# Second weight halves cast and subtracted later, the triangular inverse with two result buffers and two block loads, attention's suffix sums 0.03 of a period later

## Chip, core and metric

One core of a Trainium2 chip runs the whole program. The metric is the device time of one launch in microseconds (us); three runs of the kernel before gave 1783.5, 1784.86 and 1788.74, median 1784.86.

## What is computed

One inference step of a two-layer hybrid encoder on 512 prompt tokens and 32 sample tokens (544 columns in all), model width 1024, inner width 2048. Layer 0 is an RWKV-7 time mixer: projections of the shifted stream to r, k, v and z, a data-dependent decay, and per head (32 heads of 64) the state recurrence

```
S_t = S_(t-1) diag(w_t) - (S_(t-1) kk_t)(kk_t * a_t)^T + v_t k_t^T ;  y_t = S_t r_t
```

with a group norm, a bonus term, a SiLU gate and an output projection. Its output gives one shared key and value set. Layer 1 is stick-breaking attention with 16 heads of 128, strictly causal:

```
A[t,s] = sigmoid(z_ts) * prod over s<j<t of (1 - sigmoid(z_tj))
```

computed in log space: the suffix sums of log(1 - sigmoid) are matrix products with a triangular matrix.

## The kernel before

**Precision.** Each projection in float32 is three matmuls on a high and a low part: weight high by x high, weight high by x low, weight low by x high. The parts of a weight are made on the chip: SP loads half a column block (512 of the 1024 rows, `wraw`, four buffers), ScalarE (ACT) casts it (`whi`, line 231), and VectorE (DVE) in layer A, or GpSimd (POOL) in layer B, subtracts (`wlo`, line 232). `wsplit` takes the next of three pairs of `whi`/`wlo` buffers in a ring during layer A, so a cast waits until TensorE (PE) has done the last matmul that reads that buffer.

**Order.** All work from the recurrence on is put on an agenda: `at(t, fn)` with t in periods, one period per pair of heads in layer A (16 pairs, three stages of successive pairs overlapping) and one per head in layer B. `flush` sorts the agenda by t, and each engine gets its instructions in that order and runs them in that order. So t sets places in queues, not times. A pair's period is some 38 us in layer A; a head's is some 31 us in layer B. A few entries have small offsets in a table `SHIFT`.

**Layer A, per pair.** `plan_load` (line 530) puts the two loads of a weight block at t and t + 0.3 d, and the two splits (cast and subtract) at t + d and t + 1.47 d, d = 0.17. For the key weights (`q.kw`, t = p - 0.95) that is 0.22 and 0.30 of the period before pair p's, for the value weights (`q.vw`, t = p + 0.55) 0.72 and 0.80. `plan_proj` puts 16 quanta of three matmuls (line 560) over a slot: keys in p - 0.5 to p, values in p + 1 to p + 1.5. `plan_c` is the recurrence over chunks of 64 tokens in eight steps, each x, u, s a twenty-fourth of a period apart: x (line 907 on PE, `xs` line 918 on DVE, `sgc` line 922 on ACT), u (line 929 on PE, `vu` lines 932 and 933 on ACT), s (line 944 on PE, state `st` line 952 on DVE). Between these PE runs the quanta of the projections.

**The triangular inverse.** The recurrence needs the inverses of small unit lower triangular matrices. `plan_b` stores four 32 x 32 block sets to DRAM (`nd`, line 741, due at 0.62), loads them back with one matrix per partition (`npt`, line 754, three loads at 0.70), and POOL does 31 steps of a multiply and an add (lines 771 and 776, due from 0.79 to 1.62) in `qp`, which starts as the identity: `init` (line 764, at 0.78) copies it from `qinit`, filled once by three loads. The result goes to DRAM (`qd`, line 757, at 1.635) and from there back into `lm` (`fetch`, line 745, at 1.73). `plan_m` (transposes `mt`, line 791, on DVE; matmuls 797 and 807) uses it from 1.86 on. All transfers named here are issued by SP, in agenda order. `decays2` (line 596) makes the chunk-end decays `gc` with two small POOL copies from `gx`.

**Layer B, per head.** `plan_att`: logits, six steps of soft-plus per block of scores (last step `spl`, line 1617, DVE), then `tails` (line 1633, PE: matmuls of `sph` and `spl` with the triangle), `add` (line 1637, DVE), `weigh` (line 1640, ACT), `values` (lines 1656 to 1661, PE), and the gates (lines 1667 and 1671, DVE). PE fills in with the quanta of the next head's key, value and query projections. `split_oz` makes the parts for the output projection.

Of the kernel before, what the change touches and what calls it, by code (L numbers as in the profile page):

```python
# [9 lines left out]
F32 = mybir.dt.float32  # L10
# [13 lines left out]
DEC = 32  # L24
# [63 lines left out]
def tile_encoder(ctx: ExitStack, tc: tile.TileContext, i, o):  # L88
# [366 lines left out]
    V.tensor_scalar(out=ka1, in0=vecs["k_a"], scalar1=-1.0, scalar2=1.0, op0=ALU.mult, op1=ALU.add)  # L455
    qg = const.tile([P, 1], F32, name="qg")
    V.tensor_scalar(out=qg, in0=vecs["q_gain"], scalar1=float(P ** -0.5), scalar2=None, op0=ALU.mult)
    qinit = const.tile([108, 11, 32], F32, name="qinit")

    def identity_rows():  # L460

        idd = dram.tile([33, 32], F32, name="idd")
        SY.dma_start(idd, ident[0:33, 0:32])
        for g in range(3):
            SY.dma_start(
                qinit[36 * g:36 * g + 36],
                idd.rearrange("(i g) t -> g i t", g=3)[g:g + 1].broadcast_to([36, 11, 32]))

    def last_rows():
        hl = p1b.tile([P, 2, NK], F32, name="hl")  # L470
# [62 lines left out]
            fn(*args)  # L533
        agenda.clear()

    def plan_load(idx, t, d=0.17):

        parts = wready[idx] = [None, None]

        def load(kh):  # L540
            parts[kh] = wfetch(idx, kh)

        def split_w(kh):
            parts[kh] = wsplit(parts[kh])
        for kh in range(2):
            at(t + 0.3 * d * kh, load, kh)
            at(t + d + 0.47 * d * kh, split_w, kh)

    def plan_proj(x, idx, t0, t1, evac):

# [20 lines left out]
    def plan_a(q):  # L571
# [24 lines left out]
        def decays2():  # L596
            A.activation(q.sg, q.sg, AF.Exp, scale=KAPPA)
            q.gc = wk.tile([P, NCH], F32, tag="gc", name="gc", bufs=4)
            G.tensor_copy(q.gc[:, 0:NCH - 1], q.gx[:, 0:NCH - 1, C])
            G.tensor_copy(q.gc[:, NCH - 1:NCH], q.gx[:, NCH - 1, DEC:DEC + 1])  # L600
        at(t0 - 0.32, decays2)

        def rscaled():
# [126 lines left out]
    def plan_b(q):  # L730

        t0 = q.p
        nd, qd = nd_d[q.p], qd_d[q.p]

        def nblock(hd, b):
            r0 = 64 * (1 - hd) + 32 * b
            return q.lm[r0:r0 + 32, hd, :, 0, 32 * b:32 * b + 32]

        def store(hd, b):
            m = (2 * hd + b) * NCH  # L740
            SY.dma_start(nd[m:m + NCH].rearrange("c s t -> s c t"), nblock(hd, b))

        def fetch(hd, b):
            m = (2 * hd + b) * NCH
            SY.dma_start(nblock(hd, b), qd[m:m + NCH, 0:32].rearrange("c s t -> s c t"))
        for hd in range(2):
            for b in range(2):
                at(t0 + 0.62, store, hd, b)
                at(t0 + 1.73, fetch, hd, b)

        def load(g):
            if g == 0:
                q.npt = wk.tile([108, 32, 32], F32, tag="npt", name="npt")
            SY.dma_start(q.npt[36 * g:36 * g + 36], nd)

        def out(g):
            SY.dma_start(qd.rearrange("m (i g) t -> g m i t", g=3)[g], q.qp[36 * g:36 * g + 36])
        for g in range(3):
            at(t0 + 0.70, load, g)
            at(t0 + 1.635, out, g)  # L760

        def init():
            q.qp = wk.tile([108, 11, 32], F32, tag="qp", name="qp")
            G.tensor_copy(q.qp, qinit)
        at(t0 + 0.78, init)

        def row(j):
            ni, nt = j // 3 + 1, 31 - j
            tmp = wk.tile([108, 11, 32], F32, tag="qtmp", name="qtmp")
            q.tt = tmp[:, 0:ni, 0:nt]  # L770
            G.tensor_tensor(q.tt, q.npt[:, j, j + 1:32].unsqueeze(1).broadcast_to([108, ni, nt]),  # L771
                            q.qp[:, 0:ni, j:j + 1].broadcast_to([108, ni, nt]), ALU.mult)

        def add(j):
            ni = j // 3 + 1
            G.tensor_tensor(q.qp[:, 0:ni, j + 1:32], q.qp[:, 0:ni, j + 1:32], q.tt, ALU.add)  # L776
        b0, b1 = t0 + 0.79, t0 + 1.62
        for j in range(31):
            at(b0 + (b1 - b0) * (2 * j) / 62, row, j)
            at(b0 + (b1 - b0) * (2 * j + 1) / 62, add, j)  # L780
# [388 lines left out]
    at(1.02, open_b)  # L1169
    for p, q in enumerate(pairs):  # L1170
        if p >= 2:
            plan_load(q.kw, p - 0.95)
        if p >= 1:
            plan_load(q.vw, p + 0.55)
        for plan in (plan_a, plan_lm, plan_b, plan_m, plan_v, plan_c, plan_d):
            plan(q)

# [387 lines left out]
    def plan_att(q):  # L1565
# [78 lines left out]
            for step in range(6):  # L1644
                at(t0 + 0.185 + 0.07 * n + 0.03 * step, soft, b, step)
        for n, b in enumerate((2, 1, 0)):
            at(t0 + 0.53 + 0.035 * n, tails, b)
            at(t0 + 0.565 + 0.035 * n, add, b)
            at(t0 + 0.60 + 0.035 * n, weigh, b)
        out = {}  # L1650

        def values(n):
# [7 lines left out]
            TE.matmul(out["s"][:, :DEC], q.cv, z[2][:, 256:288], start=True, stop=False)  # L1660
            TE.matmul(out["s"][:, :DEC], q.v[:, 4], z[2][:, 288:320], start=False, stop=True)
        for n in range(4):
            at(t0 + 0.72 + 0.02 * n, values, n)
        at(t0 + 0.80, svalues)

        def gate():
            V.tensor_tensor(oz[:, j, 0:SEQ], out["p"], q.z[:, 0:SEQ], ALU.mult)  # L1667
        at(t0 + 0.83, gate)

        def sgate():  # L1670
            V.tensor_tensor(oz[:, j, SEQ:T], out["s"][:, :DEC], q.z[:, SEQ:T], ALU.mult)
        at(t0 + 0.85, sgate)

    def plan_xb():
        st = {}
# [56 lines left out]
        A.copy(hi, oz[:, j, :])  # L1732
        (V if j >= 8 else G).tensor_tensor(out=lo, in0=oz[:, j, :], in1=hi.bitcast(F32), op=ALU.subtract)  # L1733
    for j in range(NE):
        at(NE - 1 - third + 0.02 + 0.04 * j if j < 8 else NE - 1 + 0.02 + 0.04 * (j - 8) if j < NE - 1 else NE - 1 + 0.88,
           split_oz, j)
    with tc.manual_schedule():
        flush()
# [57 lines left out]
```

## Time and profile before

| | |
|---|---|
| runs, us | 1783.5, 1784.86, 1788.74 |
| the profiled execution, us | 1785.67 |
| its span, us | 1784.0 |
| mean granted clock of PE | 0.982 |
| busy: PE, weight loads, DVE, ACT, POOL | 94%, 81%, 43%, 50%, 38% |
| DMA: moved, share of 16 engines | 203.75 MB, 38.2% |
| layer A's steady part | about 270 to 770 us of the span |
| layer B's heads | about 1190 to 1690 us of the span |

Times in the rows are from the start of the span. In a timeline row come the start, the length of the piece, the engine, the line, the operation with tiles and shape, how many were merged (x4), and in brackets how long the engine had been idle before it and whose result ended that idle time. SPq is SP's queue of transfers; its lengths are the time to issue them. PE counts as busy while matmuls are under way, so small waits between them show as idle time of under a microsecond.

### The profile page before, as it was taken

The numbers are of one execution on the slowest core, as the hardware profiler recorded it, in microseconds if no ns is written. First come the engines' busy times: TensorE is split into PE (matmuls) and PEld (weight loads), VectorE is DVE, ScalarE is ACT, GpSimd is POOL, SyncE is SP. The second block draws the span as 40 slices with busy tenths as digits, with TensorE's granted clock in tenths as the row PEclk, the third lists the DMA queues.
The fourth block names the chain that finished last, engine by engine and source line by source line (L and its number), as shares of the span: only waits on it lengthen the run. The fifth ranks groups of instructions, "written<-read, shape, count | busy, mean of one in ns | idle before, by whom it ended". The sixth has DMA issues, their size and how long they took to land. (4 is left out here: it accounts for less than half of the span.)

```text
span 1784.0 us, 38442 instructions
## 1 busy us (share of the span) xinstructions
PE 1675.3 (94%) x15107; PEld 1444.3 (81%) x15107; DVE 765.6 (43%) x1564; ACT 884.9 (50%) x2232; POOL 681.4 (38%) x1371
## 2 busy tenths in 40 slices
PE   5999979999999999999989998999999999999899
PEld 2679867777777777778868998998888888888798
DVE  3674445545555545552355223123443434334400
ACT  2555545565565556555443335254554545555521
POOL 1000276656667666663002443432222222222432
PEclk8999989999999999989999999999999999999999
DMA  8457522333232333332585443433233232323232
GB/s 326 154 160 233 180 76 69 108 84 86 73 80 73 107 80 93 94 89 66 178 287 148 125 142 91 139 106 110 63 85 88 66 107 58 98 75 103 78 111 79
DMA packets 302612, 203.75 MB, mean 114 GB/s; under 512 B 79726, under 2 KB 271872, under 8 KB 300256
## 3 DMA queue, kind: packets, MB, share of 16 engines
q1 hardware_dynamic: 302432, 201.30, 38.2%
q8 instruction: 119, 1.95, 0.5%
q14 instruction: 61, 0.50, 0.1%
HBM read 155.28 MB, written 45.96 MB: 113 GB/s over the span
## 5 line engine op out<-in xcount | busy, mean ns | idle before, releaser
L560 PE MATMUL mm<-x,whi 128*128 128x272 f32 x3584 | 798.4, 315 | 7.0 <-DVE x L1274 3.5
L560 PEld LDWEIGHTS mm<-x,whi 128*128 128x128 f32 x3584 | 572.0, 191 | 70.7 <-issue 23.3
L232 POOL TENSOR_TENSOR wlo<-wraw,whi 128x512 fp32r<-128x512 f32 x198 | 255.2, 1299 | 702.1 <-ACT whi L231 702.1
L560 PE MATMUL mm<-x,wlo 128*128 128x272 f32 x1792 | 520.8, 291 | 1.7 <-POOL wlo L232 1.7
L560 PEld LDWEIGHTS mm<-x,wlo 128*128 128x128 f32 x1792 | 341.3, 190 | 2.4 <-POOL wlo L232 2.4
L231 ACT CAST whi<-wraw 128x512 fp32r<-128x512 f32 x324 | 195.1, 618 | 138.1 <-issue 78.4
L771 POOL TENSOR_TENSOR qtmp<-npt,qp 108x84 f32<-108x84 f32 (+23 forms) x496 | 194.0, 391 | 77.9 <-DMA npt<-nd_d 38.4
L776 POOL TENSOR_TENSOR qp<-qp,qtmp 108x84 f32<-108x84 f32 (+23 forms) x496 | 194.7, 393 | 37.9
L232 DVE TENSOR_TENSOR wlo<-wraw,whi 128x512 fp32r<-128x512 f32 x126 | 88.9, 707 | 116.3 <-ACT whi L231 114.6
L260 PE MATMUL mm<-x,whi 128*128 128x272 f32 x512 | 101.2, 293 | 2.8 <-POOL x L1733 1.4
L932 ACT COPY vu<-ch 64x64 f32<-64x64 f32 (+1 forms) x128 | 27.5, 215 | 133.7 <-PE ch L929 133.4
L952 DVE SCALAR_TENSOR_TENSOR st<-ch,gc,sgc 128x64 f32<-128x64 f32 x128 | 35.7, 279 | 128.2 <-PE ch L944 125.0
L260 PEld LDWEIGHTS mm<-x,whi 128*128 128x128 f32 x512 | 81.7, 190 | 3.9 <-POOL x L1733 1.8
L560 PE MATMUL mm<-xrh,whi 128*128 128x272 f32 x240 | 73.0, 304 | 1.6 <-ACT rout L1087 1.4
L260 PE MATMUL mm<-x,wlo 128*128 128x272 f32 x256 | 74.5, 291 | 0.0
L260 PE MATMUL mm<-yh,whi 128*128 128x272 f32 x256 | 73.9, 288 | 0.0
L260 PE MATMUL mm<-yh,wlo 128*128 128x272 f32 x256 | 73.8, 288 | 0.0
L260 PE MATMUL mm<-yl,whi 128*128 128x272 f32 x256 | 73.8, 288 | 0.0
L560 PE MATMUL mm<-xrh,wlo 128*128 128x272 f32 x240 | 69.3, 289 | 0.3 <-DVE wlo L232 0.3
L560 PE MATMUL mm<-xrl,whi 128*128 128x272 f32 x240 | 69.1, 288 | 0.0
L922 ACT ACTIVATE sgc<-st,gc 128x64 f32<-128x64 f32 x112 | 38.7, 346 | 46.6 <-DVE st L952 46.2
L1640 ACT ACTIVATE z<-z 128x512 f32<-128x512 f32 (+1 forms) x48 | 27.8, 579 | 68.1 <-DVE z L1637 68.1
(322 smaller groups left out, 3180.0 us busy)
## 6 DMA issues: line engine op xcount, KB each, us to landing
wraw<-in_a_w_in_dram SPq DMA_DIRECT2D x128, 256.0 KB
wraw<-in_kv_w_dram SPq DMA_DIRECT2D x68, 256.0 KB
wraw<-in_b_w_in_dram SPq DMA_DIRECT2D x64, 256.0 KB
rca<-rca_d SPq DMA_DIRECT2D x16, 816.0 KB
rca_d<-sgat SPq DMA_DIRECT2D x16, 544.0 KB
x<-in_a_ada_w_dram SPq DMA_DIRECT2D x8, 1024.0 KB
adaw<-in_b_ada_w_dram SPq DMA_DIRECT2D x8, 1024.0 KB
wraw<-in_a_w_out_dram SPq DMA_DIRECT2D x32, 256.0 KB
```

Of the source, the lines that this page charges most:

```text
L231: A.copy(hi, raw)
L232: (V if onV[0] else G).tensor_tensor(out=lo, in0=raw, in1=hi.bitcast(F32), op=ALU.subtract)
L260: TE.matmul(ps[:, :HT], a[:, k % KH, :], b[:, k, s], start=n == 0, stop=n == total - 1)
L560: TE.matmul(ps[half][:, :HT], a[:, k % KH, :], b[:, k, s], start=k + n == 0, stop=k == NK - 1 and n == 2)
L771: G.tensor_tensor(q.tt, q.npt[:, j, j + 1:32].unsqueeze(1).broadcast_to([108, ni, nt]), q.qp[:, 0:ni, j:j + 1].broadcast_to([108, ni, nt]) ...
L776: G.tensor_tensor(q.qp[:, 0:ni, j + 1:32], q.qp[:, 0:ni, j + 1:32], q.tt, ALU.add)
L922: A.activation(sg, state[c], AF.Copy, scale=q.gc[:, c:c + 1])
L932: A.copy(q.vu[64:128, cs, 0, :], pu[64:128, 0:64 * m].rearrange("p (m t) -> p m t", m=m))
L952: V.scalar_tensor_tensor(new, src, gc, ps["g", c], ALU.mult, ALU.add)
L1640: A.activation(z[b][:, :width[b]], z[b][:, :width[b]], AF.Exp)
```

## The change

- `plan_load` takes an optional due time for the second half's split. Key weights: 0.30 becomes 0.43 of the period (p - 0.70 becomes p - 0.57); value weights: 0.80 becomes 0.895. Loads and first halves stay.
- `qp` gets two buffers; `init` moves from 0.78 to 0.52 and becomes three SP loads of the identity from DRAM (`idd`) straight into `qp`, for each of the 16 pairs; the constant `qinit`, its three loads and the POOL copies go.
- `npt` becomes two tiles of 16 rows each, filled by three loads at 0.70 and three at 0.75 (the offset of the old third load no longer applies).
- The two `gc` copies go from POOL to ACT.
- In layer B tails, add, weigh, values and gates are due 0.025 to 0.03 later, and the last head's `split_oz` with them.

```diff
@@ -455,16 +455,10 @@
     V.tensor_scalar(out=ka1, in0=vecs["k_a"], scalar1=-1.0, scalar2=1.0, op0=ALU.mult, op1=ALU.add)
     qg = const.tile([P, 1], F32, name="qg")
     V.tensor_scalar(out=qg, in0=vecs["q_gain"], scalar1=float(P ** -0.5), scalar2=None, op0=ALU.mult)
-    qinit = const.tile([108, 11, 32], F32, name="qinit")
+    idd = dram.tile([33, 32], F32, name="idd")
 
     def identity_rows():
-
-        idd = dram.tile([33, 32], F32, name="idd")
         SY.dma_start(idd, ident[0:33, 0:32])
-        for g in range(3):
-            SY.dma_start(
-                qinit[36 * g:36 * g + 36],
-                idd.rearrange("(i g) t -> g i t", g=3)[g:g + 1].broadcast_to([36, 11, 32]))
 
     def last_rows():
         hl = p1b.tile([P, 2, NK], F32, name="hl")
@@ -533,7 +527,7 @@
             fn(*args)
         agenda.clear()
 
-    def plan_load(idx, t, d=0.17):
+    def plan_load(idx, t, d=0.17, second=None):
 
         parts = wready[idx] = [None, None]
 
@@ -544,7 +538,7 @@
             parts[kh] = wsplit(parts[kh])
         for kh in range(2):
             at(t + 0.3 * d * kh, load, kh)
-            at(t + d + 0.47 * d * kh, split_w, kh)
+            at(second if kh and second else t + d + 0.47 * d * kh, split_w, kh)
 
     def plan_proj(x, idx, t0, t1, evac):
 
@@ -596,8 +590,8 @@
         def decays2():
             A.activation(q.sg, q.sg, AF.Exp, scale=KAPPA)
             q.gc = wk.tile([P, NCH], F32, tag="gc", name="gc", bufs=4)
-            G.tensor_copy(q.gc[:, 0:NCH - 1], q.gx[:, 0:NCH - 1, C])
-            G.tensor_copy(q.gc[:, NCH - 1:NCH], q.gx[:, NCH - 1, DEC:DEC + 1])
+            A.copy(q.gc[:, 0:NCH - 1], q.gx[:, 0:NCH - 1, C])
+            A.copy(q.gc[:, NCH - 1:NCH], q.gx[:, NCH - 1, DEC:DEC + 1])
         at(t0 - 0.32, decays2)
 
         def rscaled():
@@ -748,27 +742,32 @@
                 at(t0 + 0.62, store, hd, b)
                 at(t0 + 1.73, fetch, hd, b)
 
-        def load(g):
+        def load(h, g):
+
             if g == 0:
-                q.npt = wk.tile([108, 32, 32], F32, tag="npt", name="npt")
-            SY.dma_start(q.npt[36 * g:36 * g + 36], nd)
+                q.npt = getattr(q, "npt", []) + [wk.tile([108, 16, 32], F32, tag=f"npt{h}", name=f"npt{h}")]
+            SY.dma_start(q.npt[h][36 * g:36 * g + 36], nd[:, 16 * h:16 * h + 16, :])
 
         def out(g):
             SY.dma_start(qd.rearrange("m (i g) t -> g m i t", g=3)[g], q.qp[36 * g:36 * g + 36])
         for g in range(3):
-            at(t0 + 0.70, load, g)
+            at(t0 + 0.70, load, 0, g)
+            at(t0 + 0.75, load, 1, g)
             at(t0 + 1.635, out, g)
 
         def init():
-            q.qp = wk.tile([108, 11, 32], F32, tag="qp", name="qp")
-            G.tensor_copy(q.qp, qinit)
-        at(t0 + 0.78, init)
+
+            q.qp = wk.tile([108, 11, 32], F32, tag="qp", name="qp", bufs=2)
+            for g in range(3):
+                SY.dma_start(q.qp[36 * g:36 * g + 36],
+                             idd.rearrange("(i g) t -> g i t", g=3)[g:g + 1].broadcast_to([36, 11, 32]))
+        at(t0 + 0.52, init)
 
         def row(j):
             ni, nt = j // 3 + 1, 31 - j
             tmp = wk.tile([108, 11, 32], F32, tag="qtmp", name="qtmp")
             q.tt = tmp[:, 0:ni, 0:nt]
-            G.tensor_tensor(q.tt, q.npt[:, j, j + 1:32].unsqueeze(1).broadcast_to([108, ni, nt]),
+            G.tensor_tensor(q.tt, q.npt[j // 16][:, j % 16, j + 1:32].unsqueeze(1).broadcast_to([108, ni, nt]),
                             q.qp[:, 0:ni, j:j + 1].broadcast_to([108, ni, nt]), ALU.mult)
 
         def add(j):
@@ -1169,9 +1168,9 @@
     at(1.02, open_b)
     for p, q in enumerate(pairs):
         if p >= 2:
-            plan_load(q.kw, p - 0.95)
+            plan_load(q.kw, p - 0.95, second=p - 0.57)
         if p >= 1:
-            plan_load(q.vw, p + 0.55)
+            plan_load(q.vw, p + 0.55, second=p + 0.895)
         for plan in (plan_a, plan_lm, plan_b, plan_m, plan_v, plan_c, plan_d):
             plan(q)
 
@@ -1644,9 +1643,9 @@
             for step in range(6):
                 at(t0 + 0.185 + 0.07 * n + 0.03 * step, soft, b, step)
         for n, b in enumerate((2, 1, 0)):
-            at(t0 + 0.53 + 0.035 * n, tails, b)
-            at(t0 + 0.565 + 0.035 * n, add, b)
-            at(t0 + 0.60 + 0.035 * n, weigh, b)
+            at(t0 + 0.56 + 0.035 * n, tails, b)
+            at(t0 + 0.595 + 0.035 * n, add, b)
+            at(t0 + 0.625 + 0.035 * n, weigh, b)
         out = {}
 
         def values(n):
@@ -1660,16 +1659,16 @@
             TE.matmul(out["s"][:, :DEC], q.cv, z[2][:, 256:288], start=True, stop=False)
             TE.matmul(out["s"][:, :DEC], q.v[:, 4], z[2][:, 288:320], start=False, stop=True)
         for n in range(4):
-            at(t0 + 0.72 + 0.02 * n, values, n)
-        at(t0 + 0.80, svalues)
+            at(t0 + 0.75 + 0.02 * n, values, n)
+        at(t0 + 0.83, svalues)
 
         def gate():
             V.tensor_tensor(oz[:, j, 0:SEQ], out["p"], q.z[:, 0:SEQ], ALU.mult)
-        at(t0 + 0.83, gate)
+        at(t0 + 0.86, gate)
 
         def sgate():
             V.tensor_tensor(oz[:, j, SEQ:T], out["s"][:, :DEC], q.z[:, SEQ:T], ALU.mult)
-        at(t0 + 0.85, sgate)
+        at(t0 + 0.88, sgate)
 
     def plan_xb():
         st = {}
@@ -1732,7 +1731,7 @@
         A.copy(hi, oz[:, j, :])
         (V if j >= 8 else G).tensor_tensor(out=lo, in0=oz[:, j, :], in1=hi.bitcast(F32), op=ALU.subtract)
     for j in range(NE):
-        at(NE - 1 - third + 0.02 + 0.04 * j if j < 8 else NE - 1 + 0.02 + 0.04 * (j - 8) if j < NE - 1 else NE - 1 + 0.88,
+        at(NE - 1 - third + 0.02 + 0.04 * j if j < 8 else NE - 1 + 0.02 + 0.04 * (j - 8) if j < NE - 1 else NE - 1 + 0.91,
            split_oz, j)
     with tc.manual_schedule():
         flush()
```

## Rows read from the trace of the kernel before

**Rows 1.** The page's first part: busy time, share of the span and number of instructions of each engine.
```profile
PE 1675.3 (94%) x15107; PEld 1444.3 (81%) x15107; DVE 765.6 (43%) x1564; ACT 884.9 (50%) x2232; POOL 681.4 (38%) x1371
```

**Rows 2.** The list of waits of PE over the whole span: who waited for whom, us in total, how often, the longest.
```profile
PE at L1633 <- DVE spl L1617: 9.1, 15, 0.6
PE aux L797 <- DVE mt L791: 7.9, 15, 5.3
```

**Rows 3.** The same list for 300 to 760 us, twelve periods of layer A.
```profile
PE ch L907 <- DVE st L952: 17.4, 13, 1.5
PE aux L797 <- DVE mt L791: 2.3, 12, 0.2
```

**Rows 4.** Timeline of one period of layer A around the old place of the key weights' second split, ACT, DVE and PE.
```profile
499.33 0.62 ACT L231 CAST whi<-wraw 128x512 fp32r<-128x512 f32 x1 [0.51 <-PE mm L560]
499.34 0.34 PE L944 MATMUL ch<-vu,kbt 128*64 128x64 f32 x4
...
499.98 0.69 DVE L232 TENSOR_TENSOR wlo<-wraw,whi 128x512 fp32r<-128x512 f32 x1 [1.15 <-ACT whi L231]
...
500.59 0.88 DVE L666 TENSOR_TENSOR rk<-rca,k 128x544 f32<-128x544 f32 x1
501.39 0.27 DVE L952 SCALAR_TENSOR_TENSOR st<-ch,gc,sgc 128x64 f32<-128x64 f32 x1
...
501.72 0.33 PE L907 MATMUL ch<-st,ar 64*64 64x64 f32 x4 [1.35 <-DVE st L952]
```

**Rows 5.** Timeline of PE, the same matmul in three other periods.
```profile
270.47 0.33 PE L907 MATMUL ch<-st,ar 64*64 64x64 f32 x4 [1.41 <-DVE st L952]
...
424.36 0.33 PE L907 MATMUL ch<-st,ar 64*64 64x64 f32 x4 [1.51 <-DVE st L952]
...
463.76 0.33 PE L907 MATMUL ch<-st,ar 64*64 64x64 f32 x4 [1.33 <-DVE st L952]
```

**Rows 6.** Three stretches of the span: their bounds, their length, busy time (and instructions) of PE, PE's weight loads, DVE, ACT and POOL, PE's granted clock as a share of full speed, the DMA engines' busy share, GB/s.
```profile
271.50:274.90 3.40, 3.40 (x32) 2.86 (x29) 1.29 (x2) 0.41 (x2) 2.84 (x12) 0.50 0.93 285
425.00:428.40 3.40, 3.40 (x36) 2.86 (x34) 1.68 (x4) 0.41 (x2) 2.85 (x10) 0.52 0.60 152
...
657.20:660.60 3.40, 3.40 (x36) 2.83 (x35) 1.07 (x2) 0.42 (x2) 2.77 (x11) 0.50 0.85 268
```

**Rows 7.** Timeline of the same period as Rows 4, around the new place of the key weights' second split.
```profile
504.24 0.21 ACT L933 COPY vu<-ch 64x64 f32<-64x64 f32 x1
...
505.51 0.28 DVE L952 SCALAR_TENSOR_TENSOR st<-ch,gc,sgc 128x64 f32<-128x64 f32 x1 [1.05 <-PE ch L944]
...
505.65 0.19 ACT L958 COPY yr<-aux 128x32 f32<-128x32 f32 x1 [1.20 <-PE aux L980]
...
506.10 0.33 PE L907 MATMUL ch<-st,ar 64*64 64x64 f32 x4
```

**Rows 8.** Timeline of the same period, around the old and the new place of the value weights' second split.
```profile
518.14 0.21 ACT L933 COPY vu<-ch 64x64 f32<-64x64 f32 x1
...
518.69 0.34 PE L944 MATMUL ch<-vu,kbt 128*64 128x64 f32 x4
...
519.33 0.69 DVE L232 TENSOR_TENSOR wlo<-wraw,whi 128x512 fp32r<-128x512 f32 x1 [3.10 <-ACT whi L231]
...
520.59 0.97 DVE L791 STREAM_TRANSPOSE mt<-lm 32x288 f32<-32x288 f32 x2
...
521.61 0.75 PE L797 MATMUL aux<-mt,lm 32*32 32x32 f32 x34 [0.19 <-DVE mt L791]
...
522.67 0.21 ACT L932 COPY vu<-ch 64x64 f32<-64x64 f32 x1 [1.86 <-PE ch L929]
...
524.02 0.28 DVE L952 SCALAR_TENSOR_TENSOR st<-ch,gc,sgc 128x64 f32<-128x64 f32 x1 [2.01 <-PE ch L944]
```

**Rows 9.** Timeline of SP's queue and of POOL in the same period: the inverse's transfers and its first step.
```profile
504.41 1.15 SPq L221 DMA_DIRECT2D wraw<-in_a_w_in_dram  x2
509.24 2.47 SPq L741 DMA_DIRECT2D nd_d<-lm  x4
511.81 2.52 SPq L757 DMA_DIRECT2D qd_d<-qp  x3
514.51 1.24 SPq L754 DMA_DIRECT2D npt<-nd_d  x3
516.17 1.97 SPq L745 DMA_DIRECT2D lm<-qd_d  x4
...
519.63 0.49 POOL L771 TENSOR_TENSOR qtmp<-npt,qp 108x31 f32<-108x31 f32 x1 [2.92 <-DMA npt<-nd_d]
```

**Rows 10.** The instructions of the tile `qinit`: shortest, median and longest issue in ns, first and last start in us.
```profile
L465 SPq DMA_DIRECT2D qinit<-idd x3: 342/430/435, 63.5 to 64.4; - x3
```

**Rows 11.** Timeline of the first pair's inverse: the last transfers and PE's wait for them.
```profile
245.82 1.81 SPq L745 DMA_DIRECT2D lm<-qd_d  x4
...
250.13 1.57 PE L797 MATMUL aux<-mt,lm 32*32 32x32 f32 x36 [5.27 <-DVE mt L791]
```

**Rows 12.** Timeline of PE in one head of layer B: the last quantum ahead of the suffix sums, and their first two matmuls.
```profile
1234.53 0.41 PE L560 MATMUL mm<-x,whi 128*128 128x272 f32 x2
...
1234.90 0.38 PE L1633 MATMUL at<-sph,ntri 128*128 128x256 f32 x1
1235.88 0.39 PE L1633 MATMUL at<-spl,ntri 128*128 128x256 f32 x1 [0.60 <-DVE spl L1617]
```

## The prediction

> **What bounds the kernel now.** I read the busy table first. PE is under way 94% of the span and no other engine comes to 51% [rows 1], so time goes only where PE waits, or where its clock falls. Next the list of PE's waits, whole and for the twelve steady periods of layer A. Two entries there belong to the parts that this change touches most: in layer A the matmul of line 907 waits for the state `st` for 17.4 us, 13 times, of which one is small (about 0.1) and twelve are 1.3 to 1.5 [rows 3]; in layer B the suffix sums wait 9.1 us for `spl` in 15 heads [rows 2]. The wait of line 797 for `mt` is 0.19 a period [rows 3], 7.9 in all with one of 5.3 in the first pair [rows 2].
>
> Then the timeline around one of the twelve, to see who is late [rows 4]. PE's matmul 944 for the state is over at 499.68. `st` could follow at once, but in DVE's queue ahead of it stands the subtraction of the key weights' second half. It idles 1.15 us for ACT's cast, and the cast itself had idled 0.51 us until PE had read the last of the buffer that it overwrites. So DVE, free at 498.83, does the subtraction from 499.98, then `rk` (0.88), and `st` only at 501.39; PE stands from 500.37 to 501.72. This is a wait for a buffer that has grown through two queues.
>
> Last the clock. Right after some of these waits (270.47, 424.36 [rows 5]) the granted clock is about 0.5, 1.2 GHz, for 3.4 us with PE busy throughout: I found one after the wait at 270 us and three in the steady part, first and last shown [rows 6]. From 424.36 to 463.76 [rows 5], a period with such a stretch, it takes 39.40 us; from 463.76 to 501.72 [rows 4], one without, 37.96. A stretch costs 1.44.
>
> **The change part by part.**
>
> *Key weights' second half, 0.30 to 0.43.* It now stands behind the copies of step u(3) on ACT and behind the masks on DVE, ahead of `st` of s(3). At the old place DVE does `rk` at 498.83 and `st` at about 499.7, done before 500.37, so PE does not wait: twelve waits, 17.3 us, and the one at 270.47 (pair 3's block), 1.41 [rows 3, 5]: 18.7 us. The blocks of pairs 0 and 1 keep their own due times and are not counted. At the new place ACT is free at 504.45 and would idle 1.20 [rows 7]; the buffer has been free since 499.3. Cast 0.62 [rows 4], so DVE subtracts from 505.07 to 505.76, and `st`, now at 505.51, comes at 505.76 and ends at 506.03; PE wants it at 506.10 [rows 7]. What is queued behind the split is just this `st`, and who waits for it is line 907. The margin is 0.07. Bounds: nothing, and a subtraction in full, 0.69 in each of 13 periods, 9.0. I take 0.05 each, 0.6 us, since the rows put the end ahead of the need.
>
> *The clock.* Without the waits I expect the four stretches that followed them to go: 4 x 1.44 = 5.8 us. Bounds 0 and 5.8. I take the upper, because the stretches start within a microsecond of the end of such a wait and the waits of 0.2 us that stay are a seventh as long.
>
> *Value weights' second half, 0.80 to 0.895.* Before, DVE idled 3.10 us for this cast, then subtracted for 0.69 at 519.33, and `st`, the first product and the `mt` transposes followed it, the latter at 520.59; PE waited 0.19 for them [rows 8]. Now these come about 0.9 earlier on DVE, and the transposes are held by their transfer instead, which should have landed by about 520.0 (the last is issued at 518.14 [rows 9]; the first pair's are in use 1.5 us after the last issue at most, 247.63 to 250.13 less 0.97 for the transposes [rows 8, 11]). They end at about 521.0, ahead of PE: 14 waits of 0.19, 7.9 - 5.3 = 2.6 us [rows 2]. At its new place the cast falls into 1.86 us of idle ACT and the subtraction into 2.01 us of idle DVE [rows 8]: nothing.
>
> *The chunk-end decays on ACT.* Two copies, the nearest rows are 0.19 and 0.21 [rows 7], so 0.4 us more at 0.68 of a period, where ACT has no idle time up to the copies of u(6), which end at 518.35; PE uses them at 518.69 [rows 8]. 0.34 of the 0.4 is slack; with the hand-over I take 0.1 in 15 periods, 1.5 us; bounds 0 and 6.0. The freed POOL time stands ahead of its wait for the blocks [rows 9] and gives nothing.
>
> *The inverse.* `init` by SP is three issues of 0.43 [rows 10], 1.3 us a pair, at 0.52, ahead of the weight loads and the stores. SP idles from 505.56 to 509.24 [rows 9], so the stores stay where they are. The second `qp` buffer lets it run before the old result has left. Three more issues for the second `npt` halves stand behind the fetch; POOL needs them only at its 17th step. The three loads that filled `qinit` at 63.5 us [rows 10] go; no engine waited for them, so nothing. The first halves have half the bytes: from the last issue at 515.75 to POOL's first step are 3.88 us [rows 9], small transfers take 1.5, so up to 2.3 goes with size and half of that is 1.1; I take 1.0, bounds 0 and 3.9. In the steady part this is only slack: results go out when the stores ahead of them in SP's queue are issued (509.24 + 2.47 [rows 9]), not when POOL ends. It keeps POOL's end in place as the period shrinks by 1.4. In the first pair PE stands 5.27 for the inverse [rows 11], and there it is worth its 1.0 us. The Trainium skill ("DMA: Bandwidth & Descriptors", section on the anatomy of one DMA) fits a transfer as 2.0 us fixed and the bytes at 436 GB/s; by that, halving three loads of 144 KB saves 0.5 us, an estimate, and the sum would be 0.5 us smaller. The rows leave more to size than that.
>
> *Layer B.* Of the next head's value quanta exactly one, due at 0.5417, lies between 0.53 and 0.56. It now runs ahead of the sums and takes 0.37 us (1234.53 to 1234.90 [rows 12]). The first matmul reads `sph`, ready; the second waits 0.60 for `spl` [rows 12], whose place in DVE's queue is not moved. So 0.37 of 0.60 is filled in 15 heads: 5.6 us; bounds 0 and the whole 9.1 [rows 2]. The end of the sums moves by a quantum, and values and gates are due later by the same 0.03, so their order among the quanta hardly changes. In the last head no projection is left to put between, and the order stays.
>
> **Sum**: 18.7 + 5.8 + 2.6 + 1.0 + 5.6 - 0.6 - 1.5 = 31.6 us. The profiled execution took 1785.67 (its span of 1784.0 and 1.67 around it), so 1754.1; it stands 0.8 above the median of the runs, so 1784.86 - 31.6 = **1753.3**.
>
> **The rivals.**
>
> *The clock falls all the same.* The waits go but stretches at half clock come behind other, smaller ones. For it: I know them only beside the waits. Against: even of the thirteen waits of 1.3 to 1.5 us nine had none behind them. 1753.3 + 5.8 = 1759.1.
>
> *The wait moves to the new place.* The margin of 0.07 at 506.10 is thin. If the cast finds ACT late by 0.8 there, PE waits 0.73 in 13 periods (9.5 us), and the half-clock stretches stay: 31.6 - 9.5 - 5.8 = 16.3, so 1768.6. Against: 1.20 us of idle ACT [rows 7].
>
> *Slower: the inverse returns late.* Init brings 3 x 396 pieces of 128 bytes per pair into queues that also carry the weights, the stores and the blocks. If these hold back stores or fetch, DVE waits at `mt`, with `xs` and the rest of its queue behind, and PE waits at 797 in all 15 periods. There are about 0.4 us of slack (transposes from 520.0; PE stopped for them at 521.42, so 520.4 would do [rows 8]), then each microsecond costs 15. It decides from a fetch that lands 2.5 us later, which uses up all 31.6; at 2.9 later it is 37.5, and the time 1791. Against: SP's 3.7 us of idle time ahead of the stores, and only half as many bytes ahead of the fetch. The Trainium skill (the same page, Specifications) says that transfers under 512 bytes do not run at line rate, which speaks for this case; no run here shows what a queue of them costs the others.
>
> *It doesn't do what it says.* If the second halves were late because of their loads and not of the buffer, a later due time would bring nothing in layer A but 1 us, and with layer B's 0 to 5.6 the time is 1778 to 1784. The cast's idle time ends on PE's matmul and not on a transfer [rows 4], so I give it little.
>
> **How the numbers follow.** Forecast 0.69; clock falls all the same 0.12; wait moves 0.13; no effect in layer A 0.03; slower 0.03. Low end: all 9.1 of layer B (3.5 more), no price on ACT and at the new place (2.1), and one stretch at half clock fewer in the first pairs (1.44): 1746. High end: the wait that moves: 1769. Under 0.3%, 5.4 us, cannot be told from no change. Faster by more: the first three cases, 0.94; within 0.3%: the no-effect case, 0.03; slower: 0.03.
>
> **What would show it.** Right: PE's wait for `st` in the steady part down from 17.4 to under 2 us; periods of about 36.5 us (37.96 less 1.44 and the smaller terms), all alike; no half clock between 280 and 760; PE's wait for `mt` gone but for the first pair's, which is near 4.3; the wait for `spl` at 0.2 in each head. Wrong: a wait of line 907 just after step s(3) (the moved split); DVE's transposes idle for the fetch by more than 0.5 us with PE waiting behind; line 944 waiting for `vu` by 0.3 or more (the copies on ACT); heads of layer B no shorter than before.

## The result

The changed kernel takes 1744.48 us (median of three, 1741.59 to 1745.32) against 1784.86: a ratio of 0.9751, with a 95% interval of 0.9714 to 0.9788. (This is the estimate that belongs to the interval; the quotient of the two medians is 0.9774, inside it.) The medians stand 40.4 us apart; forecast were 31.6, and 1744.48 lies 1.5 us below the low end of the range. The profiled execution took 1741.59, its span 1739.9.

### The profile page after: what moved, and what is told of

Its sections match the earlier page's. It is cut to its first block, busy times and chain, and to the rows that moved or that the text cites. A ratio compares the mean times of both kernels' runs of the same rounds, so it can differ in the third digit from the quotient of the medians.

```text
span 1739.9 us, 38572 instructions
## 1 busy us (share of the span) xinstructions
PE 1658.2 (95%) x15107; PEld 1433.8 (82%) x15107; DVE 760.8 (44%) x1564; ACT 884.2 (51%) x2264; POOL 666.7 (38%) x1323
## 4 chain that ended last, share of the span: by engine, by line
PE 74%; ACT 9%; DVE 7%; issue 4%; DMA 3%; POOL 2%; SPq 2%; ACTq 0%; DVEq 0%; POOLq 0%
PE mm L554 34%; PE mm L260 10%; PE at L1632 3%; PE at L1582 3%; PE aux L679 2%; PE aux L1655 2%; PE ch L928 2%; PE ch L943 2%; PE ch L906 2%; ACT junk L1453 2%; PE aux L839 1%; PE pada L186 1%; DVE at L1610 1%; ACT sph L1613 1%; PE aux L435 1%
## 5 line engine op out<-in xcount | busy, mean ns | idle before, releaser
L770 POOL TENSOR_TENSOR qtmp<-npt,qp 108x84 f32<-108x84 f32 (+23 forms) x496 | 190.1, 383 | 156.5 <-DMA npt<-nd_d 122.1
L775 POOL TENSOR_TENSOR qp<-qp,qtmp 108x84 f32<-108x84 f32 (+23 forms) x496 | 200.0, 403 | 37.9
```

The source lines that it names most:

```text
L770: G.tensor_tensor(q.tt, q.npt[j // 16][:, j % 16, j + 1:32].unsqueeze(1).broadcast_to([108, ni, nt]), q.qp[:, 0:ni, j:j + 1].broadcast_to( ...
```

## The profile after

In after the line numbers have moved: 907 is 906, 944 is 943, 952 is 951, 797 is 796, 791 is 790, 1633 is 1632, 560 is 554.

First the busy line of the page, to hold against [rows 1], and PE's waits: three rows of the whole list against [rows 2], then those of 300 to 740 us against [rows 3] (us in total, how often, the longest).

```profile
PE 1658.2 (95%) x15107; PEld 1433.8 (82%) x15107; DVE 760.8 (44%) x1564; ACT 884.2 (51%) x2264; POOL 666.7 (38%) x1323
```

```profile
PE at L1632 <- DVE spl L1616: 5.0, 15, 0.6
PE aux L796 <- DVE mt L790: 4.4, 2, 3.9
...
PE ch L906 <- DVE st L951: 2.9, 3, 1.8
```

```profile
PE ch L943 <- ACT vu L932: 2.1, 12, 0.2
PE ch L906 <- DVE st L951: 2.0, 2, 1.8
PE y L979 <- ACT yr L988: 1.9, 12, 0.2
PE ch L928 <- DVE xs L917: 0.3, 1, 0.3
```

The wait for `st` is down from 17.4 to 2.0, the one for `mt` is gone from the steady part, and the wait for `spl` is about halved. The 2.0 that are left (1.8 at 731.45 us and 0.2 at 737.10) aren't left from the 17.4: the kernel before has the same two waits at 767.83 and 773.50, outside the window of [rows 3]. Next, the old and the new place of the key weights' second half in one period, on ACT, DVE and PE, against [rows 4, 7].

```profile
480.52 0.88 DVE L660 TENSOR_TENSOR rk<-rca,k 128x544 f32<-128x544 f32 x1
...
481.09 0.34 PE L943 MATMUL ch<-vu,kbt 128*64 128x64 f32 x4
...
481.54 0.28 DVE L951 SCALAR_TENSOR_TENSOR st<-ch,gc,sgc 128x64 f32<-128x64 f32 x1
...
482.04 0.33 PE L906 MATMUL ch<-st,ar 64*64 64x64 f32 x4
...
484.67 0.62 ACT L231 CAST whi<-wraw 128x512 fp32r<-128x512 f32 x1
485.32 0.69 DVE L232 TENSOR_TENSOR wlo<-wraw,whi 128x512 fp32r<-128x512 f32 x1 [0.54 <-ACT whi L231]
...
485.93 0.28 DVE L951 SCALAR_TENSOR_TENSOR st<-ch,gc,sgc 128x64 f32<-128x64 f32 x1
...
486.43 0.33 PE L906 MATMUL ch<-st,ar 64*64 64x64 f32 x4
```

Neither matmul of line 906 has a bracket: PE waits at neither place. At the old place `rk` runs before PE asks; at the new one the cast follows ACT's copies at once, and `st` ends at 486.21, 0.22 ahead of PE.

The clock, as windows (bounds, length, busy time and instructions of PE, weight loads, DVE, ACT, POOL, then the granted clock, DMA share, GB/s), two of the changed kernel and then one of the kernel before:

```profile
300.00:733.00 433.00, 426.98 (x5510) 342.47 (x5509) 245.57 (x545) 268.81 (x820) 298.57 (x821) 1.00 0.41 99
733.50:743.70 10.20, 9.96 (x78) 8.29 (x74) 8.19 (x16) 4.67 (x12) 8.79 (x19) 0.50 0.29 74
```

```profile
769.90:780.10 10.20, 9.95 (x78) 8.29 (x74) 8.21 (x15) 4.68 (x12) 8.79 (x19) 0.50 0.27 84
```

Full clock from 300 to 733 us, where the kernel before had three stretches at about half, that is at 1.2 GHz instead of 2.4, two of them in [rows 6]. The stretch of 10.2 us at 733.5 isn't new: the kernel before has it at 769.9, with the same 78 matmuls; it comes earlier only because all before it takes less time. It starts 2 us behind the one large wait for `st` that is left, here in the timeline of DVE and PE, with its match in the kernel before below:

```profile
729.55 0.90 DVE L1240 TENSOR_TENSOR x<-x 128x544 fp32r<-128x544 f32 x1
730.38 0.82 DVE L232 TENSOR_TENSOR wlo<-wraw,whi 128x512 fp32r<-128x512 f32 x1
731.13 0.27 DVE L951 SCALAR_TENSOR_TENSOR st<-ch,gc,sgc 128x64 f32<-128x64 f32 x1
...
731.45 0.33 PE L906 MATMUL ch<-st,ar 64*64 64x64 f32 x4 [1.80 <-DVE st L951]
```

```profile
767.83 0.33 PE L907 MATMUL ch<-st,ar 64*64 64x64 f32 x4 [1.81 <-DVE st L952]
```

Here the mixing of z (line 1240) and the weights' subtraction stand in DVE's queue ahead of `st`. All other steady periods of layer A are alike: from one pair's `mt` product to the next PE takes 35.87 to 35.89 us. Before it was 37.9 to 38.2, and 39.5 to 39.6 with a stretch at half clock. Measured from the start of one matmul to the start of the next (start to start, below), the 2.07 us that a period without such a stretch loses are 1.42 at the old wait of line 907, 0.44 at the `mt` product and 0.16 at line 907 of step x(7). The idle time ahead of the `mt` product had shown 0.19 [rows 3, 8]. In layer B a head goes from 31.40 to 31.02; its two rows against [rows 12]:

```profile
1258.27 0.28 PE L1632 MATMUL at<-sph,ntri 128*128 128x256 f32 x1
1258.86 0.39 PE L1632 MATMUL at<-spl,ntri 128*128 128x256 f32 x1 [0.31 <-DVE spl L1616]
```

## The experiments

Open after this: the value weights' part seemed worth three times its forecast, and the inverse's parts showed next to nothing of their own. So each part was put alone into the kernel before.

**Keys alone.**

```diff
...
-            at(t + d + 0.47 * d * kh, split_w, kh)
+            at(second if kh and second else t + d + 0.47 * d * kh, split_w, kh)
...
-            plan_load(q.kw, p - 0.95)
+            plan_load(q.kw, p - 0.95, second=p - 0.57)
```

> The kernel before with one part: the key weights' second half split at p - 0.57. By the forecast: 18.7 us of waits, 5.8 of half clock, less 0.6 at the new place, so 23.9 us less, about 1761. By the revised theory, drawn from the changed kernel's trace: 13 waits of 1.42 (18.5) and the half-clock stretches behind them (1.44 each, four), nothing at the new place, so 24 to 25 us less, 1760 to 1761, if the waits go without the other parts' help. Rival (the parts need each other: with the mt transposes still 0.6 us late and POOL's init in its old place, PE's clock or the state's chain loses again what the keys win): less than 20 us, above 1765.

Measured: ratio 0.9856 (0.9833 to 0.9880), so 25.7 us less (21.4 to 29.8; here and below such figures are the ratio's share of 1784.86). The trace gives 22.4 in 284 to 764 us, that is between the two matmuls that PE starts at these times in the kernel before and the same two here (so in the next sections too), and 2.95 at pair 3, with no wait for `st` and no stretch at half clock between 280 and 740 us. The part carries itself.

**Values alone.**

```diff
...
-            plan_load(q.vw, p + 0.55)
+            plan_load(q.vw, p + 0.55, second=p + 0.895)
```

> The kernel before with one part: the value weights' second half split at p + 0.895. By the forecast 14 x 0.19 = 2.6 us less, about 1782. By the revised theory the idle time shown ahead of line 797 understates this part: the starts of PE's instructions moved together by 0.44 a period at the mt transposes' readers, and by 0.16 at line 907 of step x(7), so 14 x 0.60 = 8.4 us less, about 1776.5. Rival (those 0.60 come from the shorter period or the faster inverse, not from this split): under 4 us less, above 1781.

Measured: 0.9934 (0.9912 to 0.9957), 11.8 us less (7.7 to 15.7). PE's waits for 300 to 740 us:

```profile
PE ch L907 <- DVE st L952: 16.2, 12, 1.5
PE ch L944 <- ACT vu L933: 2.2, 12, 0.2
PE y L980 <- ACT yr L989: 1.8, 11, 0.2
PE aux L797 <- DVE mt L791: 0.2, 1, 0.2
```

The wait for `mt` goes, that for `st` stays. Start to start, in 284 to 764 us, 5.06 come at the `mt` product and 3.3 at line 907: 8.4, as expected. The rest, some 3, are stretches at half clock: this execution has one there and that of the kernel before three; whether that is chance isn't shown.

**The inverse alone** (two buffers, start values by SP, blocks in two loads; the decays stay on POOL; the diff is that of the change).

> The kernel before with one part: the inverse in two buffers, its start values written by SP, its blocks in two loads; the chunk-end decays stay on POOL. By the forecast 1.0 us less, from the first pair. By the revised theory 1.0 to 3: the first pair's gap at line 797 (5.27 to about 4.3, since in the changed kernel it is 3.93 and 0.43 with the other parts) and, if that gap is what set the long half-clock stretch behind it, up to 1.7 more. Rival (the start values' 128-byte pieces hold back the weights or the stores, as long as the second halves are at their old places): slower than before by 1 us or more.

Measured: 0.9974 (0.9961 to 0.9988), 4.6 us less (2.1 to 7.0). By the trace 2.7 of it are in the first pair and 2.2 in the next 15 us; from 284 to 764 us it gains nothing (-0.3). That is more than the 1.0 of the forecast, all of it ahead of the steady part; the executions also differ there in their stretches at half clock (17.0 us before, 10.2 here, between 225 and 280 us).

**Attention alone** (the due times of the change).

> The kernel before with one part: attention's sums, values and gates 0.03 of a period later. Forecast 15 x 0.37 = 5.6 us less, about 1779; by the changed kernel's trace 5.9 in layer B, with the wait for spl at 0.31 a head instead of 0.60. Both theories agree here; this checks that layer B's part adds to the others and has no side in layer A, where nothing may change.

Measured: 0.9971 (0.9951 to 0.9992), 5.2 us less (1.4 to 8.7), 5.7 of them in layer B by the trace, and nothing from 284 to 764 us (-1.8, with a stretch at half clock more).

The four singles add to 47.3, the change gives 44.4 by its ratio (37.8 to 51.0). That looks like a plain sum. It isn't:

**Both splits, nothing else.**

> The kernel before with both second halves split later and nothing else: no second buffer for the inverse, its start values and the chunk-end decays on POOL, attention as before. If the two parts add, as the revised theory has it: 25.8 and 13.2 us as each gave alone, 39 us less by their medians, or 18.5 + 2.95 + 8.4 + the half-clock stretches by their traces, 34 to 39 us less, 1748 to 1753. Rival (at the shorter period the inverse in one buffer returns too late, and the mt transposes wait for their fetch, so the values' part is lost again): 8 us or more short of that, above 1757, with idle time of DVE at the mt transposes that ends on the fetch in the steady part, and PE's wait for mt above 0.3 a period.

Measured: 0.9909 (0.9893 to 0.9925), 1770.62 us: 16.2 us less where the two alone make 37.5. The rival was right on the time and on the waits; the single buffer, which it named as the cause, is tested below. PE's waits for 300 to 740 us, then DVE's at the transposes:

```profile
PE aux L797 <- DVE mt L791: 8.8, 21, 1.2
```

```profile
DVE mt L791 <- DMA lm<-qd_d: 13.6, 11, 1.8
```

The results come back late. Why, SP's queue and POOL show:

```profile
461.91 2.01 SPq L741 DMA_DIRECT2D nd_d<-lm  x4
...
465.15 0.23 POOL L776 TENSOR_TENSOR qp<-qp,qtmp 108x11 f32<-108x11 f32 x1
...
465.41 2.52 SPq L757 DMA_DIRECT2D qd_d<-qp  x3
468.10 1.24 SPq L754 DMA_DIRECT2D npt<-nd_d  x3
...
469.82 0.48 POOL L764 COPY qp<-qinit 108x352 f32<-108x352 f32 x1 [3.61 <-DMA qd_d<-qp]
472.86 0.24 POOL L771 TENSOR_TENSOR qtmp<-npt,qp 108x31 f32<-108x31 f32 x1 [2.56 <-DMA npt<-nd_d]
```

The stores are issued by 463.92, but the results go out only at 465.41, right behind POOL's last step (to 465.38); before they had followed the stores by 0.1 [rows 9]. The next blocks are issued behind them, the next steps start when those land, and end 29 us later, when results go out again: a ring. Two parts of the change could shorten it, the second buffer and the halved blocks. Each was undone in the changed kernel.

**Blocks whole again.**

```diff
...
-            SY.dma_start(q.npt[h][36 * g:36 * g + 36], nd[:, 16 * h:16 * h + 16, :])
+            SY.dma_start(q.npt[36 * g:36 * g + 36], nd)
...
-            at(t0 + 0.70, load, 0, g)
-            at(t0 + 0.75, load, 1, g)
+            at(t0 + 0.70, load, g)
...
```

> The changed kernel with the inverse's blocks in one load of 32 columns again; two buffers, start values by SP and the rest as changed. Open is which part of the inverse it is without which the two splits together gave 16 us and not 39. Theory A (the ring on POOL: results out, blocks in, 32 steps, results out): with whole blocks POOL's first step came 7.5 us after the issue of the results, with halves 5.8, and the steps take 29.3; so the ring is 36.8 with whole blocks and 35.1 with halves, against PE's 35.87. Then this kernel is slower than the changed one by about as much as both splits alone fell short, 16 to 23 us: 1760 to 1767, periods of 36.8 or more, and PE's wait for mt 8 us in the steady part. Theory B (the second buffer: the start values wait for the results to leave): no change, about 1745.

**One buffer again.**

```diff
...
-            q.qp = wk.tile([108, 11, 32], F32, tag="qp", name="qp", bufs=2)
-            for g in range(3):
-                SY.dma_start(q.qp[36 * g:36 * g + 36], ...)
-        at(t0 + 0.52, init)
+            q.qp = wk.tile([108, 11, 32], F32, tag="qp", name="qp")
+            G.tensor_copy(q.qp, qinit)
+        at(t0 + 0.78, init)
```

> The changed kernel with the inverse in one buffer again, its start values copied on POOL at 0.78 as before; blocks in two loads and the rest as changed. Theory A (halved blocks shorten the ring): the copy ends at about 4.9 us after the results' issue, before the blocks at 5.8, so it is not on the ring, and the time is that of the changed kernel, 1743 to 1747. Theory B (the second buffer): 1760 or more, with POOL's first step right behind the copy and the period above 36.5.

Measured: whole blocks 1760.50 (0.9857, 0.9834 to 0.9879), 16 us behind the changed kernel; one buffer 1744.63 (0.9766, 0.9744 to 0.9788), its time. So it is the halves. PE's wait for `mt` with whole blocks is 6.1 us in 300 to 740 us, where theory A had said 8. SP and POOL in one period, whole blocks first, then one buffer, then the changed kernel:

```profile
503.62 0.23 POOL L773 TENSOR_TENSOR qp<-qp,qtmp 108x11 f32<-108x11 f32 x1
...
503.87 2.53 SPq L751 DMA_DIRECT2D qd_d<-qp  x3
506.59 1.27 SPq L748 DMA_DIRECT2D npt<-nd_d  x3
...
511.38 0.24 POOL L768 TENSOR_TENSOR qtmp<-npt,qp 108x31 f32<-108x31 f32 x1 [7.49 <-DMA lm<-qd_d]
```

```profile
495.49 2.54 SPq L758 DMA_DIRECT2D qd_d<-qp  x3
498.21 1.24 SPq L755 DMA_DIRECT2D npt<-nd_d  x3
...
499.92 0.48 POOL L766 COPY qp<-qinit 108x352 f32<-108x352 f32 x1 [6.53 <-DMA qd_d<-qp]
501.26 0.24 POOL L773 TENSOR_TENSOR qtmp<-npt,qp 108x31 f32<-108x31 f32 x1 [0.86 <-DMA npt<-nd_d]
```

```profile
492.62 2.52 SPq L752 DMA_DIRECT2D qd_d<-qp  x3
495.32 1.27 SPq L749 DMA_DIRECT2D npt<-nd_d  x3
...
498.40 0.24 POOL L770 TENSOR_TENSOR qtmp<-npt,qp 108x31 f32<-108x31 f32 x1 [7.39 <-DMA npt<-nd_d]
```

With whole blocks the results again go out as POOL's last step ends (503.85). From their issue to POOL's first step are 7.51, 5.77 and 5.78 us. The blocks are issued 2.7 us behind the results in all three; what differs is the time from the end of their last issue to the first step, 3.5 us with whole blocks and 1.8 with halves. (The bracket of the first step with whole blocks names the fetch of the results, `lm`, which was the last to land before it; what the step reads is `npt`.) With one buffer the copy of the start values ends at 500.40, still ahead of the first step. The same from all pairs whose results go out between 280 and 760 us, as medians over 13 pairs, in us (steps: from the start of the first to the end of the last; ring: the sum of the two):

| kernel | results' issue to first step | steps | ring | mean period |
|---|---|---|---|---|
| before | 7.66 | 29.12 | 36.8 | 38.4 |
| keys alone | 7.66 | 28.60 | 36.3 | 36.6 |
| values alone | 7.73 | 29.45 | 37.2 | 37.5 |
| both splits | 7.88 | 29.19 | 37.1 | 37.4 |
| blocks whole | 7.79 | 29.30 | 37.1 | 37.5 |
| one buffer | 5.79 | 29.15 | 34.9 | 35.9 |
| changed | 5.99 | 29.19 | 35.2 | 35.9 |

With both splits PE's own work wants 35.87. With one of them alone the period is still a little above the ring, so each could gain by itself. Of the last four kernels, those with a shorter ring have the period of 35.9; the two with a longer one have the ring and a little more. That excess goes with stretches at half clock: both splits alone have three between 284 and 750 us, of 6.8, 10.2 and 6.8 us, the kernel with whole blocks three, of 6.8, 10.2 and 10.2. Where such a stretch has held PE up, POOL is ahead for a while, and single periods fall under the ring: with whole blocks two of 35.87 and 35.86 follow the one that has the first stretch.

**The decays back on POOL.**

```diff
-            A.copy(q.gc[:, 0:NCH - 1], q.gx[:, 0:NCH - 1, C])
-            A.copy(q.gc[:, NCH - 1:NCH], q.gx[:, NCH - 1, DEC:DEC + 1])
+            G.tensor_copy(q.gc[:, 0:NCH - 1], q.gx[:, 0:NCH - 1, C])
+            G.tensor_copy(q.gc[:, NCH - 1:NCH], q.gx[:, NCH - 1, DEC:DEC + 1])
```

> The changed kernel with the chunk-end decays back on POOL. By the forecast the two copies on ACT cost 1.5 us, so this one would be 1.5 us faster, 1743. By the revised theory (0.19 us of ACT for both together, inside 0.34 of slack) nothing: within 1 us of the changed kernel, and PE's wait of line 943 for vu the same 0.17 a period.

Measured: 0.9760 (0.9738 to 0.9781), against the changed kernel's 0.9751 no difference; within the intervals 1.5 us would not show, but its trace has every steady period at 35.87 to 35.90 as well. So the copies on ACT cost nothing that a period shows.

**What is left: the mixing of z, and attention once more.**

```diff
...
-            at(15.15 + 0.04 * k, mixed, k)
+            at(15.3 + 0.045 * k, mixed, k)
```

> The changed kernel with the eight mixing steps of z (a cast on ACT, a subtraction of about 0.75 us on DVE) due at 15.30 + 0.045k instead of 15.15 + 0.04k. If they are what makes the state late at 729 us: the gaps there (1.80, 0.31 and 0.24 us) go, 2.3 us less; if the half-clock stretch of 10.2 us that starts 2 us behind them comes of them too, 4.3 more, so 6.6 less, 1738. Rival (DVE is crowded there by its other work, or the first projection of z comes too late): no gain, or a wait of line 554 for x after 739 us and a slower kernel.

```diff
...
-            at(t0 + 0.56 + 0.035 * n, tails, b)
+            at(t0 + 0.57 + 0.035 * n, tails, b)
```

> The changed kernel with attention's three groups of suffix sums 0.01 of a period later still, so that one more quantum of the next head's values (0.37 us) runs ahead of them. The reading that a quantum there fills what is left of the wait for spl (0.31 a head) gives 15 x 0.31 = 4.6 us less, 1740. Rival (the sums' own end sets the end of the head, so that the quantum only changes places): no gain, with a wait of about 0.3 a head somewhere behind (exponentials, values).

Measured: 1740.37 (0.9748, 0.9728 to 0.9768) and 1737.68 (0.9731, 0.9710 to 0.9752). The intervals overlap the changed kernel's; the traces tell more. With the mixing later, what lies between 284 and 764 us in the changed kernel takes 4.74 less, of the 6.6 expected, and has no stretch at half clock; PE's longest wait for `st` in 700 to 760 us is 0.8:

```profile
PE ch L906 <- DVE st L951: 1.7, 3, 0.8
```

With the sums later, a head takes 30.64 instead of 31.02, and of the wait for `spl` in 1190 to 1640 us this is left:

```profile
PE at L1632 <- DVE spl L1616: 0.2, 1, 0.2
```

That is 0.38 a head where the idle time had shown 0.31. The rival (the sums' end sets the head) fell. Both together:

> The changed kernel with the mixing steps of z later (15.30 + 0.045k) and attention's sums 0.01 later. By the traces of each alone 4.7 us in layer A and 5.1 in layer B; if they add, 1744.5 - 9.8, about 1735. If part of the 4.7 was the chance of the half-clock stretch, 1738.

Measured: 1733.51 (0.9707, 0.9685 to 0.9729). And three more moves in layer B, against the changed kernel:

```diff
...
-            at(t0 + 0.12 + 0.04 * n, logits, b)
+            at(t0 + 0.13 + 0.04 * n, logits, b)
...
-            at(t0 + 0.56 + 0.035 * n, tails, b)
-            at(t0 + 0.595 + 0.035 * n, add, b)
-            at(t0 + 0.625 + 0.035 * n, weigh, b)
+            at(t0 + 0.59 + 0.035 * n, tails, b)
+            at(t0 + 0.62 + 0.035 * n, add, b)
+            at(t0 + 0.645 + 0.035 * n, weigh, b)
...
-            plan_k(q, j - 1, j - 2 * third, j - 2 * third + 0.03)
+            plan_k(q, j - 1, j - 2 * third, j - 2 * third + 0.05)
```

> As the one before, and in layer B three more moves by a quantum of projection each: logits at 0.13 (PE's wait for qT, 0.23 a head), the transposes of kT at 0.05 of a third (wait for kT, 0.40 a head), sums at 0.59. If each wait is filled: 15 x (0.23 + 0.37) = 9 us less than that one, about 1726. Rival: the softmax chain starts 0.37 later a head and the wait for spl comes back by 0.2 or more, 1730 to 1735.

Measured: 1727.43 (0.9680, 0.9656 to 0.9704), faster than the kernel before and the changed kernel, and 6.1 us below the last by the medians, though their intervals overlap. A head takes 30.06 instead of 30.64. PE's waits in 1190 to 1640 us begin with

```profile
PE aux L1408 <- DVE kT L1444: 5.2, 13, 0.4
```

so the move of the transposes of `kT` missed its wait, and the wait for `qT` (3.1 us in 13 heads in the changed kernel) is gone. In one head the idle time fell by that 0.23 alone, and the head by 0.58. Start to start, 0.39 of it come ahead of the logits, where the wait for `qT` was, and 0.21 at two places in the suffix sums where no idle time was shown; the sum is as expected, but for `kT` it was luck.

## Why the prediction was short

*The step that failed is the value weights' second half.* The prediction sized it by the idle time ahead of the product, 14 x 0.19 = 2.6 us. Alone it gave 11.8 (7.7 to 15.7), of which the trace shows 8.4 at two places: 0.42 a period at the product, from start to start, and the rest at line 907, whose matmul in x(7) and whose wait for `st` both came a little earlier. The mechanism was right (the split stood ahead of `st`, the first product and the transposes); its size was read from the wrong column, and line 907 was not counted. This is most of why the period came to 35.87 and not to about 36.5.

*Key weights' second half and the clock*: 18.7 + 5.8 - 0.6 = 23.9 forecast, 25.7 (21.4 to 29.8) measured alone. Right, and by its mechanism: the stretches behind those waits went with them. (They start 0.7 to 1.7 us behind the end of the wait, the latter at 657.2 after a wait to 655.53, not all within a microsecond.) The charge of 0.6 at the new place did not come.

*The decays on ACT*: 1.5 charged, nothing measured. The two copies, of 0.20 and 0.19, start 0.10 apart (495.07 and 495.17 in the changed kernel's timeline), so together they take 0.29, and the cast behind them starts 0.19 after the first (495.26); both are inside the 0.34 of slack. Adding the copies up as 0.4 was wrong.

*The inverse*: 1.0 in the first pair, "in the steady part this is only slack". As a single part that holds (nothing in the steady part; 2.7 in the first pair). In the change it does not, and this is a second step that failed: without the halves the kernel takes 1760.50, 16 us more. The slack was read at a period of 38, where results wait for the stores; the prediction's own period of 36.5 was already below the ring of 36.8. The prediction did say that the halves keep POOL's end in place as the period shrinks by 1.4, but it neither added up the ring nor gave a price for it. That the terms for the two splits could be added was luck: the halves, priced at 1.0, were what let them. The Trainium skill ("DMA: Bandwidth & Descriptors", the anatomy of one DMA) gave 0.5 us for the halving, an estimate; the way from results to first step became 1.7 shorter (7.66 to 5.99), so the trace does not agree with it here. The section's fit is for transfers that GpSimd issues, and these are issued by SP, so it was the wrong one to take.

*Layer B*: 5.6 forecast, 5.2 (1.4 to 8.7) alone. The head is 0.38 shorter with 0.37 put in, though the idle time ahead of `spl` fell to 0.31 and not to 0.2.

*The rivals.* The clock did not fall all the same: the stretch at 733 us, behind the mixing of z, is the one at 769.9 in the kernel before. The prediction had not looked there, so its sign "no half clock between 280 and 760" failed for a stretch that the change does not touch and only brings forward. The wait did not move to the new place: `st` is 0.22 ahead. "The inverse returns late" was the right worry with the wrong cause: not SP's small pieces, which the kernel with one buffer does without at the same time, but the round trip of the blocks, which the change had shortened by more than was needed (a ring of 35.2 against a period of 35.87).

What stays open: 40.4 by the medians or 44.4 by the ratio; the charges not met (2.1), the values (5.8 beyond forecast) and the shorter first pair (its longest wait went from 5.3 to 3.9, and the stretch at half clock behind it from 10.2 to 6.8 us) cover the 8.8 between forecast and medians, but how many stretches at half clock one execution has is partly chance, so this does not split exactly.

## What to carry to other kernels

Slack is worth what it is at the new period: before a wait is taken out of a loop, add up every ring that comes back through a queue (results out, blocks in, steps) and compare it with the period that is hoped for. Measure a wait from start to start of the instructions on both sides, not by the idle time shown alone: in this profile the ends of matmuls are modelled. Parts whose single gains add up to the whole can still depend on each other: undo each from the finished kernel as well.

## What the runs showed of the hardware

- A wait cost more than its idle time: 0.44 for 0.19 shown (`mt`), 0.38 for 0.31 (`spl`), 0.39 for 0.23 (`qT`), 1.42 for 1.35 (`st`).
- Three loads of 72 KB in place of 144 KB ahead of a first step brought it 1.7 to 2.1 us nearer to the issue of the results ahead of them (medians 7.66 to 7.88 against 5.79 to 5.99).
- Stretches at half clock in layer A's steady part came behind PE's waits, for `st` (424.36 us, before) as for `mt` (550.05, whole blocks), and not behind each: twelve waits of 1.3 to 1.5 were followed by one in the steady part in one execution (values alone) and by three in another (before). 23 executions of the kernel before, on one chip, took 1779.95 us with a mean granted clock of 0.986 to 1793.74 with 0.977.
